# Residual and normalised activations on VectorE in 512-column pieces, with half units, ordered splits and paced scatters

## The chip, the cores and the metric

The kernel runs on one core of a Trainium2 chip. The metric is the device time of one execution in microseconds (us), the median of several runs; less is better. The engines are TensorE (PE; its weight loads are shown as PEld), VectorE (DVE), ScalarE (ACT), GpSimd (POOL) and SyncE (SP, which here only issues loads and stores). GpSimd issues DMAs too, among them all gathers and scatters by index.

## The reference

One decoder layer for 256 tokens of width 2048, with 16 learned meta tokens ahead of them (272 positions), all in float32:

```python
h = layer_norm(concat(meta, x))
proj = h @ w_in                      # 9264 columns: pool, z, x, B, C, dt
mix = concat(pool_mix(...), ssd_mix(...)) @ w_out
h = layer_norm(ALPHA * h + mix)
h = layer_norm(ALPHA * h + peer_ffn(h))

def peer_ffn(xb):                    # 16384 experts of one neuron
    q = (xb @ wq)                    # 8 heads, two halves of 128
    # top 16 of 128 keys per half, top 16 of the 256 pairs, softmax -> gate
    act = gelu(xb . u_tab[expert])
    return (gate * act) @ v_tab[expert]
```

The meta tokens are dropped from the output.

## The kernel before

Every large matrix product is done in three passes over pairs of fp32r numbers: each weight and each activation is split into a high part (a rounded copy) and a low part (the rest), and high x high, high x low and low x high are added up in PSUM. A weight unit is 128 x 1024 numbers. `next_unit` (L114) keeps three units ahead of the one in use: SP loads the raw unit (L124), ScalarE casts it to `wh` (L127), VectorE subtracts to get `wl` (L128). `raw`, `wh` and `wl` have three buffers each. W_ORDER (L79 to L109) is the list in which units come, and it must match the order of use. So each unit costs ScalarE and VectorE one instruction each, and TensorE waits if one of these is late.

The stages, with their places in the trace:

1. *Start (to about 25 us).* x is loaded and normalised without gain and bias (L198 to L231). For each of 16 chunks of 128 columns, TensorE transposes it and `normed_T` (L178) applies gain and bias and splits it into `hTH` and `hTL`: one or two instructions on ScalarE and one or two on VectorE per chunk.
2. *Input projection and mixers (to 506 us).* `mm_unit` (L251) multiplies half of the contraction (8 chunks, 24 matmuls) by one unit; `proj` (L259) calls it for both halves and after each half calls `tick`, which runs one step of the list `side`. All smaller work is written as generators on that list.
3. *Output projection (506 to 701 us).* `wide_pass` (L475) goes twice (dh) over 32 units, with 12 matmuls of 512 columns per unit. In the first pass, at unit 20, `w_out_body` (L506) loads the two norm vectors, broadcast to all partitions (1 MB each), and x again (two tiles `h`, 1 MB each), and rebuilds the normalised input as the residual: VectorE subtracts the mean and scales, GpSimd multiplies by the gain and adds the bias, each on a whole 128 x 2048 tile. Then it loads the vectors of the next norm into the same buffers:

```python
dve.tensor_scalar(h, h, mv_in[:, tt, 0:1], rs_in[:, tt:tt + 1], ALU.subtract, ALU.mult)
pool.tensor_mul(h, h, gb[0])
pool.tensor_add(h, h, gb[1])
```

4. *First LayerNorm (701 to about 740 us).* Statistics, scaling, then transposes and `normed_T` for 16 chunks into `h1H` and `h1L` (L568 to L572).
5. *Query projection (to 825 us)* with 16 pairs of units (L848); routing steps run from `side`. The first entry on it, `nat_steps` (L577), multiplies and adds gain and bias to the normalised tiles on GpSimd, whole tiles again, and stores them to `h1d` in DRAM from GpSimd's queue, for the last residual.
6. *u blocks (825 to 1607 us).* 128 blocks of 128 experts, two units each, Gelu, gating. The gating multiplies on GpSimd (L734). Three steps of `side` run per block until the routing is done; from then on the gating of the first half is spread over the blocks left to 62. Then the active rows of the coefficients are scattered to DRAM (`acd`) so that rows in use come close together: `scatter` (L690) is an indirect DMA on GpSimd, one per 128 experts, behind the last pinned instruction on that queue. From the time when positions are known, three of the other half (`scatter_0`) go out after each u block, beside those of the first half.
7. *Expert stage (1607 to 2112 us).* 107 blocks: two dense ones, whose coefficients stay in SBUF, and 105 that are read back. For each, `rows` (L952) loads a coefficient tile `ac` on SP and gathers 128 rows of v (1 MB) by index into `rawv` on GpSimd; the gather is pinned to program order. `rawv` has three buffers, `ac` seven. The halves of a row go through the same casts and subtractions as weights. `a_split` (L966) splits the coefficients on ScalarE and VectorE when a block comes up. A block multiplies both token tiles (24 matmuls) or one (12). After each of the early blocks, two more `scatter_0` are issued (L1057). `vp`, the pool of these buffers, is opened in the space of `ap1`, the half buffer `a_half[1]`, which is closed just ahead of it (L935). The residual is reloaded from `h1d` on GpSimd's queue before the stage (L933).

The framework orders the instructions of each engine by priority (the order of the program) and by when their operands are ready by its own model; an instruction named in `keep_in_program_order` keeps its place. Each engine then runs its list strictly in order, so one that waits holds up all behind it.

```python
while next_got[0] < min(i + 1 + GA, near[0]):
    k = next_got[0]
    half, blk, _ = V_BLOCKS[k]
    got[k], acs[k] = rows(acd[half][blk * P:(blk + 1) * P, :], "rawv", "ac", GA, GA + 4)
    next_got[0] += 1
```

## Time and profile before

| | |
|---|---|
| time, median of 3 runs | 2144.62 us (2144.24 to 2146.91) |
| profiled execution, its own time | 2123.32 us |
| its span, first to last instruction | 2121.6 us |
| mean granted TensorE clock | 0.982 |
| TensorE busy (matmuls) | 2031.5 us, 96%, 14780 instructions |
| VectorE | 1592.9 us, 75% |
| ScalarE | 1114.5 us, 53% |
| GpSimd | 570.7 us, 27% |
| HBM read and written | 407.2 and 21.1 MB, 202 GB/s over the span |

All rows come from one profiled execution. Busy time is an average over stages with different limits; what a change is worth is read in its own stage. A window gives the busy time of each engine in a stretch, with the number of instructions. In the timeline, neighbouring instructions of one kind are merged ("x4"), and the bracket gives the idle time of the engine before them and what ended it. Matmuls overlap, so the time of a group of them is longer than the step to the next group.

### The profile page before, as it was taken

The numbers are of one execution on the slowest core, as the hardware profiler recorded it, in microseconds if no ns is written. First come the engines' busy times: TensorE is split into PE (matmuls) and PEld (weight loads), VectorE is DVE, ScalarE is ACT, GpSimd is POOL, SyncE is SP. The second block draws the span as 40 slices with busy tenths as digits, with TensorE's granted clock in tenths as the row PEclk, the third lists the DMA queues.
The fourth block names the chain that finished last, engine by engine and source line by source line (L and its number), as shares of the span: only waits on it lengthen the run. The fifth ranks groups of instructions, "written<-read, shape, count | busy, mean of one in ns | idle before, by whom it ended". The sixth has DMA issues, their size and how long they took to land. (4 is left out here: it accounts for less than half of the span.)

```text
span 2121.6 us, 37592 instructions
## 1 busy us (share of the span) xinstructions
PE 2031.5 (96%) x14780; PEld 1867.4 (88%) x14780; DVE 1592.9 (75%) x2500; ACT 1114.5 (53%) x1637; POOL 570.7 (27%) x433
## 2 busy tenths in 40 slices
PE   7999999999899699999999999999997999998997
PEld 6999999998688599999999999999996778776775
DVE  7767777777654868999899879999754556565667
ACT  6457777776243444445558663333443445454553
POOL 1000000000400400000555426566275733222330
PEclk9999999999999799999999999999999999999999
DMA  5555555555566355555455556656687987677774
GB/s 174 183 175 175 175 175 175 175 175 196 212 202 196 116 187 180 176 182 180 151 168 171 168 179 195 200 182 206 203 263 255 306 304 282 245 271 265 268 271 156
DMA packets 113972, 430.76 MB, mean 203 GB/s; under 512 B 14113, under 2 KB 27809, under 8 KB 98801
## 3 DMA queue, kind: packets, MB, share of 16 engines
q1 hardware_dynamic: 88880, 280.19, 42.8%
q0 software_dynamic: 24624, 147.62, 19.3%
q8 instruction: 116, 1.90, 0.3%
q14 instruction: 64, 0.52, 0.1%
q10 hardware_dynamic: 288, 0.52, 0.1%
HBM read 407.20 MB, written 21.09 MB: 202 GB/s over the span
## 5 line engine op out<-in xcount | busy, mean ns | idle before, releaser
L127 ACT CAST wh<-raw 128x1024 fp32r<-128x1024 f32 (+1 forms) x502 | 525.5, 1047 | 668.8 <-PE psu L256 334.6
L128 DVE TENSOR_TENSOR wl<-raw,wh 128x1024 fp32r<-128x1024 f32 (+1 forms) x502 | 638.3, 1274 | 280.0 <-ACT wh L127 276.6
L989 PE MATMUL psv<-wh,v_scr 128*128 128x512 f32 x1304 | 365.1, 401 | 31.4 <-ACT wh L127 28.4
L128 DVE TENSOR_TENSOR wl<-rawv,wh 128x1024 fp32r<-128x1024 f32 x210 | 252.8, 1223 | 140.4 <-ACT wh L127 138.1
L734 POOL TENSOR_TENSOR o<-oe,gT 128x512 f16<-128x512 f16 x128 | 204.4, 1608 | 481.5 <-DVE gT L845 273.2
L989 PEld LDWEIGHTS psv<-wh,v_scr 128*128 128x128 f32 x1304 | 247.8, 191 | 96.5 <-ACT wh L127 36.1
L127 ACT CAST wh<-rawv 128x1024 fp32r<-128x1024 f32 x210 | 215.9, 1047 | 149.2 <-PE psv L989 90.1
L256 PE MATMUL psu<-h1H,wh 128*128 128x256 f32 x2048 | 292.9, 286 | 0.0
L256 PE MATMUL psu<-h1L,wh 128*128 128x256 f32 x2048 | 286.1, 282 | 0.0
L256 PE MATMUL psu<-h1H,wl 128*128 128x256 f32 x2048 | 284.4, 282 | 0.0
L256 PEld LDWEIGHTS psu<-h1H,wh 128*128 128x128 f32 x2048 | 261.5, 189 | 0.0
L256 PEld LDWEIGHTS psu<-h1L,wh 128*128 128x128 f32 x2048 | 261.4, 189 | 0.0
L256 PEld LDWEIGHTS psu<-h1H,wl 128*128 128x128 f32 x2048 | 261.0, 188 | 0.0
L956 POOL DMA_INDIRECT rawv<-in_v,ac x105 | 135.2, 1288 | 299.1 <-DVE wl L128 234.4
L989 PE MATMUL psv<-wl,v_scr 128*128 128x512 f32 x652 | 209.9, 401 | 1.0
L256 PE MATMUL psj<-hTH,wh 128*128 128x272 f32 (+5 forms) x1168 | 174.3, 292 | 0.0
L692 POOL DMA_INDIRECT acd<-a,flags x126 | 149.2, 1184 | 74.8 <-DVE a L595 32.5
L256 PE MATMUL psj<-hTH,wl 128*128 128x272 f32 (+5 forms) x1168 | 166.0, 284 | 0.0
L256 PE MATMUL psj<-hTL,wh 128*128 128x272 f32 (+5 forms) x1168 | 165.9, 284 | 0.0
L989 PEld LDWEIGHTS psv<-wl,v_scr 128*128 128x128 f32 x652 | 123.1, 191 | 36.5 <-DVE wl L128 8.6
L256 PEld LDWEIGHTS psj<-hTH,wh 128*128 128x128 f32 (+1 forms) x1168 | 152.9, 188 | 2.2
L256 PEld LDWEIGHTS psj<-hTL,wh 128*128 128x128 f32 (+1 forms) x1168 | 151.7, 187 | 0.1
(252 smaller groups left out, 2310.5 us busy)
## 6 DMA issues: line engine op xcount, KB each, us to landing
raw<-in_u SPq DMA_DIRECT2D x256, 512.0 KB, 4.0
raw<-in_w_in SPq DMA_DIRECT2D x144, 512.0 KB, 3.6
raw<-in_w_out SPq DMA_DIRECT2D x64, 512.0 KB, 4.2
raw<-in_wq SPq DMA_DIRECT2D x32, 512.0 KB, 3.8
ac<-acd SPq DMA_DIRECT2D x105, 128.5 KB, 4.5
clb<-cd POOLq DMA_DIRECT2D x8, 816.0 KB, 4.5
x<-in_x SPq DMA_DIRECT2D x4, 512.0 KB, 6.2
gb<-in_ln_nat POOLq DMA_DIRECT2D x2, 1024.0 KB, 6.8
```

Source lines behind the costliest of these rows:

```text
L127: act.copy(wh[:, :n], raw[:, :n])
L128: dve.tensor_sub(wl[:, :n], raw[:, :n], wh[:, :n].bitcast(F32))
L256: pe.matmul(ps[:m, :n], w[:, k * m:(k + 1) * m], xx[:, kh * 8 + k, t0:], start=first and k == 0, stop=last and k == 7)
L692: i = pool.indirect_dma_start(out=acd[half][:, :], out_offset=bass.IndirectOffsetOnAxis(ap=pos[half][:, b:b + 1], axis=0), in_=a_half[half ...
L734: behind[0] = pool.tensor_mul(o1, oe.unsqueeze(2).to_broadcast([P, 4, 2, 64]), gT[:, t0:t0 + 4, :].unsqueeze(3).to_broadcast([P, 4, 2, 64]))
L956: i = pool.indirect_dma_start(out=raw, out_offset=None, in_=v[:, :], in_offset=bass.IndirectOffsetOnAxis(ap=ac.bitcast(U32)[:, T:T + 1], a ...
L989: pe.matmul(po[tt][n], mm[:, tt * P:(tt + 1) * P], w[:, c:c + 512], start=first, stop=end)
```

## The change

Seven edits in one kernel.

- `w_out_body`: the residual is rebuilt on VectorE alone, by `h_steps`: two scalar_tensor_tensors on each of four pieces of 512 columns, for two tiles, one piece per tick. The loads of the next norm's vectors move from unit 20 to unit 31, behind a drain.
- `nat_steps`: multiply and add on VectorE in pieces of 512 columns, eight steps instead of four, and the stores to `h1d` go to SP's queue.
- Start: after chunk 7, the first halves of the dt unit and of two projections run, before the transposes of chunks 8 to 15; `proj` takes up their PSUM tiles from `pre`. The same after chunk 7 of the first LayerNorm, with the first halves of three query units (NQ1). W_ORDER follows.
- Scatters: from u block 123 on, `scatter_0` isn't called; in the expert stage it is called from block 2 on.
- Reloads of `h1d`: behind block 8 of the expert stage.
- `ac` loads: in a loop of their own, two blocks ahead of the gathers.
- `a_split`: for block i + 1 in block i, with both instructions pinned to program order.

```diff
-    W_ORDER = [w_dt[kh] for kh in range(2)]
-    W_ORDER += [w_in[j, kh] for j in range(72) for kh in range(2)]
+    W_ORDER = [w_dt[0], w_in[0, 0], w_in[1, 0], w_dt[1], w_in[0, 1], w_in[1, 1]]
+    W_ORDER += [w_in[j, kh] for j in range(2, 72) for kh in range(2)]
     W_ORDER += [w_out[k * P:(k + 1) * P, dh * 1024:(dh + 1) * 1024] for dh in range(2) for k in range(32)]
-    W_ORDER += [wq[j, kh] for j in range(16) for kh in range(2)]
+    W_ORDER += [wq[j, kh] for kh in range(2) for j in range(NQ1)]
+    W_ORDER += [wq[j, kh] for j in range(NQ1, 16) for kh in range(2)]
     W_ORDER += [u[b, kh] for b in range(P) for kh in range(2)]
...
+            if k == KC // 2 - 1:
+
+                for t0, m in ((0, NH), (14, P), (14, P)):
+                    ps = ps_tile("psj")
+                    mm_unit(ps, hTH, hTL, 0, m, L - t0, t0)
+                    pre.append((t0, ps))
...
-        ps = ps_tile("psj")
-        for kh in range(2):
-            mm_unit(ps, hTH, hTL, kh, m, L - t0, t0)
+        if pre:
+            was, ps = pre.pop(0)
+            assert was == t0
             tick()
+        else:
+            ps = ps_tile("psj")
+            mm_unit(ps, hTH, hTL, 0, m, L - t0, t0)
+            tick()
+        mm_unit(ps, hTH, hTL, 1, m, L - t0, t0)
+        tick()
         return ps
...
-    ps = ps_tile("psj")
-    for kh in range(2):
-        mm_unit(ps, hTH, hTL, kh, NH, L)
+    _, ps = pre.pop(0)
+    mm_unit(ps, hTH, hTL, 1, NH, L)
...
+    def h_steps(tt, h, gb):
+        for c in range(4):
+            cs = slice(c * 512, (c + 1) * 512)
+            dve.scalar_tensor_tensor(h[:, cs], h[:, cs], mv_in[:, tt, 0:1], gb[0][:, cs], ALU.subtract, ALU.mult)
+            dve.scalar_tensor_tensor(h[:, cs], h[:, cs], rs_in[:, tt:tt + 1], gb[1][:, cs], ALU.mult, ALU.add)
+            yield
...
-                dve.tensor_scalar(h, h, mv_in[:, tt, 0:1], rs_in[:, tt:tt + 1], ALU.subtract, ALU.mult)
-                pool.tensor_mul(h, h, gb[0])
-                pool.tensor_add(h, h, gb[1])
+                side.append(h_steps(tt, h, gb))
                 hs.append(h)
                 sts.append(lp.tile([P, 4, 6], F32, name=f"sts{tt}"))
+        if i == 31:
+            drain()
             for q in range(2):
-                gb1.append(lp.tile([P, D], F32, tag=f"gb{q}", name=f"g1b{q}"))
+                gb1.append(lnp[0].tile([P, D], F32, tag=f"gb{q}", name=f"g1b{q}"))
                 pool.dma_start(gb1[q], ln_nat[2 + q:3 + q, :].partition_broadcast(P))
...
+        if k == KC // 2 - 1:
+            for j in range(NQ1):
+                pre.append(ps_tile("psq1"))
+                mm_unit(pre[j], h1H, h1L, 0, P, T)
...
         for tt in range(2):
-            pool.tensor_mul(hs[tt], hs[tt], gb1[0])
-            yield
-            pool.tensor_add(hs[tt], hs[tt], gb1[1])
-            pool.dma_start(h1d[tt], hs[tt])
-            yield
+            for c in range(4):
+                cs = slice(c * 512, (c + 1) * 512)
+                dve.tensor_mul(hs[tt][:, cs], hs[tt][:, cs], gb1[0][:, cs])
+                dve.tensor_add(hs[tt][:, cs], hs[tt][:, cs], gb1[1][:, cs])
+                yield
+            nc.sync.dma_start(h1d[tt], hs[tt])
...
-        ps = ps_tile("psq1")
-        for kh in range(2):
-            mm_unit(ps, h1H, h1L, kh, P, T)
+        if j < NQ1:
+            ps = pre[j]
             tick()
+        else:
+            ps = ps_tile("psq1")
+            mm_unit(ps, h1H, h1L, 0, P, T)
+            tick()
+        mm_unit(ps, h1H, h1L, 1, P, T)
+        tick()
...
-            if pos[0] is not None:
+            if pos[0] is not None and b < 123:
                 for _ in range(3):
                     scatter_0()
...
-    for tt in range(2):
-        pool.dma_start(rr[tt], h1d[tt])
...
-        while next_got[0] < min(i + 1 + GA, near[0]):
-            k = next_got[0]
-            half, blk, _ = V_BLOCKS[k]
-            got[k], acs[k] = rows(acd[half][blk * P:(blk + 1) * P, :], "rawv", "ac", GA, GA + 4)
+
+        end = min(i + 1 + GA, near[0])
+        while next_ac[0] < min(end + 2, len(V_BLOCKS)):
+            half, blk, _ = V_BLOCKS[next_ac[0]]
+            assert half or n_sc[0] == HALF[0][1]
+            acs[next_ac[0]] = load_ac(acd[half][blk * P:(blk + 1) * P, :], "ac", GA + 4)
+            next_ac[0] += 1
+        while next_got[0] < end:
+            got[next_got[0]] = rows(acs[next_got[0]], "rawv", GA)
             next_got[0] += 1
         return got[i]
...
-    def rows(src, rtag, atag, rb, ab, pin=True):
-        ac = vp.tile([P, ROW], F32, tag=atag, name="ac", bufs=ab)
+    def load_ac(src, tag, bufs):
+        ac = vp.tile([P, ROW], F32, tag=tag, name="ac", bufs=bufs)
         nc.sync.dma_start(ac, src)
-        raw = vp.tile([P, D], F32, tag=rtag, name=rtag, bufs=rb)
+        return ac
+
+    def rows(ac, tag, bufs, pin=True):
+        raw = vp.tile([P, D], F32, tag=tag, name=tag, bufs=bufs)
         i = pool.indirect_dma_start(out=raw, out_offset=None, in_=v[:, :],
                                     in_offset=bass.IndirectOffsetOnAxis(ap=ac.bitcast(U32)[:, T:T + 1], axis=0))
         if pin:
             tc.keep_in_program_order(i)
             behind[0] = i
-        return raw, ac
+        return raw
...
-        split(ah[:, c], al[:, c], src[:, c])
-        return ah, al
+
+        tc.keep_in_program_order(act.copy(ah[:, c], src[:, c]))
+        tc.keep_in_program_order(dve.tensor_sub(al[:, c], src[:, c], ah[:, c].bitcast(F32)))
+        a_ops[i] = ah, al
...
-        ah, al = a_split(i) if what == "d" else (None, None)
+        if i == 0:
+            a_split(0)
+        if i + 1 < len(V_BLOCKS):
+            a_split(i + 1)
         for dh in range(2):
-            wh, wl = next_unit()
-            if ah is None:
-                ah, al = a_split(i)
-            ops = (ah, al, wh, wl)
+            ops = (*a_ops[i], *next_unit())
...
-        for _ in range(2):
+        for _ in range(2 if i > 1 else 0):
             scatter_0()
+        if i == 8:
+            for tt in range(2):
+                pool.dma_start(rr[tt], h1d[tt])
```

## Rows read from the trace of the kernel before

**Rows 1.** The page, parts 1 and 2: busy time of each engine; TensorE's clock by slice.

```profile
PE 2031.5 (96%) x14780; PEld 1867.4 (88%) x14780; DVE 1592.9 (75%) x2500; ACT 1114.5 (53%) x1637; POOL 570.7 (27%) x433
...
PEclk9999999999999799999999999999999999999999
```

**Rows 2.** Windows: stretch, length, busy us (instructions) by engine, clock, DMA share, GB/s.

```profile
520.00:549.00 29.00, 29.00 (x128) 23.98 (x129) 15.55 (x19) 12.56 (x15) 2.81 (x5) 1.00 0.83 312
738.00:760.00 22.00, 22.00 (x181) 22.00 (x180) 10.06 (x10) 9.96 (x13) 0.00 (x0) 0.96 0.62 196
1010.00:1210.00 200.00, 196.68 (x2005) 195.08 (x2004) 187.04 (x195) 130.50 (x254) 106.82 (x66) 0.99 0.54 164
```

**Rows 3.** Windows of the projection's matmuls alone (tile pso).

```profile
550.00:592.00 42.00, 31.02 (x110) 0.84 0.51 173
```

**Rows 4.** Timelines, output projection: start, us, engine, line, out<-in, count [idle before].

```profile
551.01 5.52 POOL L520 TENSOR_TENSOR h<-h,gb 128x2048 f32<-128x2048 f32 x1 [26.34 <-DVE h L519]
...
557.53 18.80 DVE L128 TENSOR_TENSOR wl<-raw,wh 128x1024 fp32r<-128x1024 f32 x5
584.26 3.73 DVE L128 TENSOR_TENSOR wl<-raw,wh 128x1024 fp32r<-128x1024 f32 x3 [7.92 <-ACT wh L127]
...
563.11 2.07 PE L482 MATMUL pso<-wl,mixH 128*128 128x512 f32 x4 [5.21 <-DVE wl L128]
```

**Rows 5.** Timeline of the first LayerNorm.

```profile
697.09 0.68 DVE L548 SCALAR_TENSOR_TENSOR h<-h,pso 128x512 f32<-128x512 f32 x1
...
713.52 9.18 POOL L579 TENSOR_TENSOR h<-h,g1b 128x2048 f32<-128x2048 f32 x2 [11.58 <-PE pst L571]
713.60 9.38 DVE L187 TENSOR_TENSOR h1L<-full,h1H 128x256 fp32r<-128x256 f32 x2
...
722.67 9.39 POOL L581 TENSOR_TENSOR h<-h,g1b 128x2048 f32<-128x2048 f32 x2
```

**Rows 6.** Windows of the query projection's matmuls alone (tile psq).

```profile
701.50:740.10 38.60, 12.07 (x64) 0.69 0.24 87
740.10:760.00 19.90, 19.70 (x166) 1.00 0.59 185
```

**Rows 7.** Window of TensorE at the start.

```profile
11.00:24.60 13.60, 13.23 (x48) 1.00 0.38 133
```

**Rows 8.** Windows of the expert stage's matmuls alone (tile psv).

```profile
1607.00:1640.00 33.00, 20.91 (x78) 0.84 0.74 262
1640.00:1840.00 200.00, 196.51 (x836) 1.00 0.83 289
...
1860.00:1950.00 90.00, 87.40 (x362) 1.00 0.75 265
1950.00:1970.00 20.00, 13.29 (x47) 0.74 0.61 208
1970.00:2090.00 120.00, 115.19 (x483) 0.99 0.80 284
```

**Rows 9.** Timeline, start of the expert stage.

```profile
1608.04 0.42 DVE L595 TENSOR_TENSOR a_dense<-a,psu 128x256 f32<-128x256 f32 x1
...
1614.45 80.72 SPq L954 DMA_DIRECT2D ac<-acd  x22
...
1618.04 0.64 PE L989 MATMUL psv<-wl,v_scr 128*128 128x512 f32 x2
...
1630.06 2.93 PE L989 MATMUL psv<-wh,v_scr 128*128 128x512 f32 x6 [11.38 <-ACT wh L127]
```

**Rows 10.** Waits of the expert stage: engine, line, waited for, us, times, longest.

```profile
ACT v_scr L175 <- DMA ac<-acd: 82.7, 28, 10.5
...
ACT wh L127 <- DMA rawv<-in_v,ac: 56.3, 33, 4.4
...
PE psv L989 <- ACT wh L127: 28.4, 15, 11.4
```

**Rows 11.** DMA issues, 1500 to 1700 us: the gathers, median us to landing.

```profile
rawv<-in_v,ac POOLq DMA_INDIRECT x18, 8.4
```

More of the change, by code (lines that the diff above doesn't have):

```diff
@@ L24 @@
 NL1 = 3
+NQ1 = 3
 NLB = 4
@@ L195, in tile_layer, with mm_unit @@
     hTL = hTp.tile([P, KC, L], F32R, name="hTL")
+    def mm_unit(ps, xh, xl, kh, m, n, t0=0):
+        wh, wl = next_unit()
+        for w, xx, first, last in ((wh, xh, kh == 0, False), (wh, xl, False, False), (wl, xh, False, kh == 1)):
+            for k in range(8):
+                pe.matmul(ps[:m, :n], w[:, k * m:(k + 1) * m], xx[:, kh * 8 + k, t0:],
+                          start=first and k == 0, stop=last and k == 7)
+    pre = []
     with tc.tile_pool(name="ln0", bufs=1) as lp:
@@ L249, in tile_layer @@
     pool.memset(ones, 1.0)
-    def mm_unit(ps, xh, xl, kh, m, n, t0=0):
-        wh, wl = next_unit()
-        for w, xx, first, last in ((wh, xh, kh == 0, False), (wh, xl, False, False), (wl, xh, False, kh == 1)):
-            for k in range(8):
-                pe.matmul(ps[:m, :n], w[:, k * m:(k + 1) * m], xx[:, kh * 8 + k, t0:],
-                          start=first and k == 0, stop=last and k == 7)
     def proj(t0, m=P):
-        ps = ps_tile("psj")
-        for kh in range(2):
-            mm_unit(ps, hTH, hTL, kh, m, L - t0, t0)
+        if pre:
+            was, ps = pre.pop(0)
+            assert was == t0
             tick()
+        else:
[4 more added lines that the diff above has]
+        tick()
         return ps
@@ L941, in tile_layer @@
     next_got = [NDB]
+    next_ac = [NDB]
     def gathered(i):
-        while next_got[0] < min(i + 1 + GA, near[0]):
-            k = next_got[0]
-            half, blk, _ = V_BLOCKS[k]
-            got[k], acs[k] = rows(acd[half][blk * P:(blk + 1) * P, :], "rawv", "ac", GA, GA + 4)
+        end = min(i + 1 + GA, near[0])
[6 more added lines that the diff above has]
+            got[next_got[0]] = rows(acs[next_got[0]], "rawv", GA)
             next_got[0] += 1
         return got[i]
-    def rows(src, rtag, atag, rb, ab, pin=True):
-        ac = vp.tile([P, ROW], F32, tag=atag, name="ac", bufs=ab)
+    def load_ac(src, tag, bufs):
+        ac = vp.tile([P, ROW], F32, tag=tag, name="ac", bufs=bufs)
         nc.sync.dma_start(ac, src)
-        raw = vp.tile([P, D], F32, tag=rtag, name=rtag, bufs=rb)
+        return ac
+    def rows(ac, tag, bufs, pin=True):
+        raw = vp.tile([P, D], F32, tag=tag, name=tag, bufs=bufs)
         i = pool.indirect_dma_start(out=raw, out_offset=None, in_=v[:, :],
@@ L960, in rows @@
             behind[0] = i
-        return raw, ac
+        return raw
     near = [len(V_BLOCKS)]
     a_n = [0]
+    a_ops = {}
     def a_split(i):
@@ L999, in v_rest @@
                 for tt, first in ((0, e - s), (1, nblk - s)):
-                    raw, ac = rows(acd[half][bass.ds(i * P + first * P, P), :], "rawl", "acl", 1, 1, False)
+                    ac = load_ac(acd[half][bass.ds(i * P + first * P, P), :], "acl", 1)
+                    raw = rows(ac, "rawl", 1, False)
                     ah, al = (v_scr[:, 2 * tt + q, tt * P:(tt + 1) * P] for q in range(2))
@@ L1045, in tile_layer @@
                 gb2.append(g2)
-        ah, al = a_split(i) if what == "d" else (None, None)
+        if i == 0:
+            a_split(0)
+        if i + 1 < len(V_BLOCKS):
+            a_split(i + 1)
         for dh in range(2):
-            wh, wl = next_unit()
-            if ah is None:
-                ah, al = a_split(i)
-            ops = (ah, al, wh, wl)
+            ops = (*a_ops[i], *next_unit())
             if i not in LATE:
```

## The prediction

> **What bounds the kernel now.** I read the busy shares of the engines and the granted clock first [rows 1]. TensorE is busy for 96% of the span, and its granted clock is below nine tenths in one of 40 slices only. [...] Next I counted matmuls in stretches: a stretch in which TensorE never waits gives the dense rate, and the count missing elsewhere gives the loss with the slow clock included.
>
> The output projection runs 128 matmuls in 29 undisturbed us, 4.4 per us [rows 2]. From 550 to 592 us it holds 110 [rows 3] where 42 us would take 185: 75/4.4 = **17.0 us lost**. The timeline shows why [rows 4]: while GpSimd runs 128x2048 multiplies and adds of some 5.5 us each, five weight splits on VectorE take 18.80 us together, where three take 3.73 a little later. TensorE waits 5.21 us for one of them and restarts at half speed (2.07 us for four matmuls, where four dense ones need 0.9).
>
> At the first LayerNorm the pattern is plainer [rows 5]. GpSimd's two multiplies and two adds (9.18 and 9.39 us) each hold up a pair of VectorE subtractions (9.38 us for two). The window from 701.5 to 740.1 us holds 64 matmuls; at the 166 per 19.9 us behind it, 64 take 7.7 us [rows 6]. **30.9 us are lost**, of which 2 x 9.3 = 18.6 lie under GpSimd's four instructions; the rest is the chain through statistics, transposes and evictions, and a cold restart.
>
> At the start TensorE is busy 13.23 of the 13.6 us before its first projection [rows 7]: little to win.
>
> In the expert stage 836 matmuls fill 196.5 busy us, 4.25 per us [rows 8]. Each row less its count/4.25 gives the loss: 33 - 78/4.25 = 14.6 us at its start (1607 to 1640), 3.3 us to 1840, 4.8 us (1860 to 1950), 8.9 us (1950 to 1970), 6.4 us (1970 to 2090). At its start [rows 9] the first coefficient load (ac) is issued at 1614.45 us and the first gathered matmul comes at 1630.06, after 11.38 us of waiting. Later ScalarE waits for ac loads with its splits, 82.7 us in 28 waits, and the weight casts queue behind it; TensorE's own waits for casts sum to 28.4 us [rows 10].
>
> **The change part by part.**
>
> *Residual preparation (w_out_body, h_steps).* Two VectorE tensor_scalars and four GpSimd instructions go; 16 scalar_tensor_tensors on 128x512 come, at 0.68 us as that form took [rows 5]: 10.9 us on VectorE. One tick per weight unit brings two, 1.36 us, beside a split of about 1.2 in the 2.7 us of a unit (12 matmuls at 4.4 per us). That is 95% if the pieces stay where they are emitted; hoisted earlier they meet a VectorE busy 15.55 of 29 us [rows 2]. The two norm-vector loads (1 MB each) move eleven units later on GpSimd's queue and meet the weight loads there; 520 to 549 us bore 4 MB of such loads beside dense matmuls [rows 2], so I cost them at nothing, and at 3 us if the weight prefetch runs dry. Of 17.0 us I expect **16** back (13 to 17).
>
> *First LayerNorm.* nat_steps on VectorE, 16 pieces at 0.68 = 10.9 us over the first eight query units, where VectorE idles 12 of 22 us [rows 2]. The 18.6 us of blocking go, less the 1 us or so that the subtractions need themselves. Three half units (72 matmuls, 72 x 0.12 = 8.6 us) can run while chunks 8 to 15 are evicted, which fills 1 to 3 us more. **19** (15 to 22). The two stores of h1d move to SP's queue, two issues there; the weight loads behind them may start late, by nothing up to 3 us, inside the lower end.
>
> Cutting is itself charged. The row gives 0.68 us for 512 columns. [...] The idle VectorE time in [rows 2] covers the 22 us of pieces in my sum; without the cover 22 us return.
>
> *Ticks.* nat_steps takes eight ticks where it took four, so at three per block the gating starts 4/3 blocks later, and the same steps fall on fewer blocks, with VectorE already busy 187 of 200 us [rows 2]. Cost 0 to 3; I take **-1**.
>
> *Start.* Dense TensorE leaves nothing: **0**. Bounds +2, and -4 if casts for the next units, waiting for a weight buffer, stand before evictions of chunks 8 to 15 on ScalarE.
>
> *Expert stage, start.* With b < 123, 15 scatters (five blocks, three each) leave the end of the u blocks, and the two reloads (rr, 2 MB) wait until block 8, so the first half's last scatter follows its own block and no longer a queue. But the gather buffers lie in the space of the half buffer that the last u block still reads, at 1608.04 us [rows 9]. From the first ac issue to the first gathered matmul it takes 15.6 us now, with rr beside; from 1608.5 that is 1624, or 1622 without rr, against dense matmuls that end at 1618.7. The wait shrinks from 11.4 to some 4 us: with the slow restart after it **8** of 14.6 (5 to 14).
>
> *Expert stage, rest.* The ac loads go out two blocks earlier on SP and the splits stay in program order on ScalarE and VectorE, a block ahead: no cast stands behind a split whose load is late. Of 4.8 + 8.9 + 6.4 = 20.1 us I take **14** (8 to 19); the rest stays because a gather lands in 8.4 us [rows 11] and ScalarE waits 56.3 us for gathers too [rows 10]. Fifteen more scatters and the rr reload, 4 MB, now pass at 0.83 DMA share: at the row's 289 GB/s 14 us of transfer, against a headroom of 0.17 x 90 us = 15 over the 21 blocks in which they pass (18 matmuls on average, 4.3 us) [rows 8]. Cost 0 to 6, **-3**; nothing below zero is excluded, since the same scatters leave before block 49 in both kernels.
>
> **Sum**: 16 + 19 - 1 + 0 + 8 + 14 - 3 = 53 us. The profiled execution took 2123.3 us, 21.3 us (1.0%) less than the median of the runs, 2144.6; nothing in its trace says where the runs lose that. Profiled: 2070; against the median: 2144.6 - 53 = **2091.6**, say 2091.
>
> **Rivals.**
>
> *Gathers set the pace.* The waits for ac go, but TensorE meets waits for gathers instead: for it, the 8.4 us landing beside 2.8 us for a one-sided block (12 matmuls), and the 56.3 us; against it, those waits seldom reach TensorE now. The stage then yields 5 at its start and loses the 3: 16 + 19 - 1 + 5 - 3 = 36, 2109 us. Chance 0.2.
>
> *VectorE fills up.* The pieces become ready together when their loads land and run as blocks in front of splits (8 x 0.68 = 5.4 us, twice a stage). For it: 95% occupancy by emission; against: the gaps in [rows 2]. Half of 35 is lost: 53 - 17 = 36, 2109 us. Chance 0.1.
>
> *Slower.* Pinned splits turn into the wait themselves: each split must follow program order on two engines, so ScalarE stops at it in every block. Price: the mean wait, 82.7/28 = 2.95 us, in 105 blocks, of which 28.4/82.7 reaches TensorE, is 106 us, in place of the 28.4 us that stand there now. The other parts give 34, so the net is 106 - 28 - 34 = 44 us slower, 2189. It decides from (34 + 28)/105 = 0.6 us of TensorE waiting per block. Against it: with the split a block ahead and ac two blocks earlier its operand has landed before the cast's own gather. Chance 0.05.
>
> *It does not do what it says.* The framework orders instructions by readiness; the half units may change nothing. That costs 0 to 3 us of the 19, inside the forecast. That nothing at all changes has 0.02: GpSimd's long instructions are gone whatever the order.
>
> **How the numbers follow.** The forecast's own case has 0.63. All lower bounds: 13 + 15 - 3 - 4 + 5 + 8 - 6 = 28, 2117 us. All upper: 17 + 22 + 2 + 14 + 19 = 74, 2071. Both extremes at once are unlikely, but the runs' 21 us above the profile is unexplained and may not return in full, so I put the low end at 2064 and the high end at 2115, which takes in the first two rivals. A measurement of this kernel tells about 0.2% (4.3 us) from no change. Faster 0.93, within it 0.02, slower 0.05.
>
> **What would show it.** Right: no GpSimd instruction of 4 us or more in the output projection and LayerNorm, subtractions at 0.4 us, 550 to 592 us at 4.4 matmuls per us; query matmuls dense by about 722; a first gathered matmul within 6 us of the dense blocks' last one; ScalarE's waits for ac near zero. Wrong: TensorE waits for casts behind gathers as large as now, splits delayed in rows of pieces, or a gap between chunks 7 and 8 at the start.

## The result and the profile after

The changed kernel takes 2090.36 us (median, 2082.15 to 2096.47), before 2145.76 in the same comparison: a ratio of 0.9739, interval 0.9704 to 0.9774. The forecast was 2091. The sum came out, but its terms did not all: two were too small in opposite directions. So the hit to within 1 us is in part luck. The 21 us that the profiled execution of before lacked most likely have a cause of their own, which the profile after shows. One execution in the record that is set apart as slow, one of e7's four below, is left out of its median.

The page of the changed kernel, parts 1 and 2, to be set beside [rows 1]:

```profile
PE 2025.3 (97%) x14780; PEld 1868.7 (90%) x14780; DVE 1571.0 (75%) x2530; ACT 1116.7 (53%) x1637; POOL 525.2 (25%) x423
...
PEclk9999999999999999999999999999989999999999
```

Shares hardly move: 97% for 96%. The answers are in the stages.

**Output projection**, its matmuls alone, the stretch that answers to [rows 3] (the stage begins 3.3 us later):

```profile
553.00:595.00 42.00, 40.87 (x181) 1.00 0.70 237
```

181 matmuls where 110 were, at a clock of 1.00: 181/42 = 4.3 per us, nearly the dense 4.4. GpSimd runs nothing here but its DMA issues.

**First LayerNorm.** VectorE's timeline, then the query projection's windows, for [rows 5] and [rows 6]:

```profile
691.75 0.68 DVE L607 TENSOR_TENSOR h<-h,g1b 128x512 f32<-128x512 f32 x1
...
698.38 1.09 DVE L189 TENSOR_TENSOR h1L<-full,h1H 128x256 fp32r<-128x256 f32 x3
...
704.50 0.68 DVE L607 TENSOR_TENSOR h<-h,g1b 128x512 f32<-128x512 f32 x1
```

```profile
688.60:712.90 24.30, 13.30 (x83) 0.79 0.21 65
712.90:732.00 19.10, 19.10 (x163) 1.00 0.86 291
```

Three subtractions take 1.09 us where two took 9.38. The loss between the stages is 24.3 - 83/8.34 = 14.3 us, where it was 30.9. The first row of the timeline shows something that stands in the way of more: eight pieces of the residual run between 691.75 and 706.1 us, inside the chain of statistics, transposes and evictions, 8 x 0.68 = 5.4 us of VectorE. How much of it TensorE pays for is open; its waits for the scaled tiles there sum to 5.3 us, where before has 4.1.

**Start.** TensorE's timeline:

```profile
19.48 2.38 PE L204 MATMUL psj<-hTH,wh 128*48 128x272 f32 x8 [0.20 <-ACT hTH L185]
...
22.15 2.77 PE L204 MATMUL psj<-hTH,wh 128*128 128x258 f32 x11 [0.29 <-ACT wh L129]
...
37.14 1.93 PE L204 MATMUL psj<-hTH,wh 128*48 128x272 f32 x13 [0.65 <-ACT hTH L185]
```

The dense stretch of [rows 7] now has waits, two for evictions and one for a cast of weights for the half units. The output projection begins at 509.8 us, 3.3 later than the 506.5 of before.

**u blocks**, the 130 us in which the gating begins. The window of TensorE's u matmuls in the changed kernel, then the same stretch of before, counted from the first u matmul (150 to 280 us behind it):

```profile
945.80:1075.80 130.00, 113.56 (x915) 0.99 0.52 156
```

```profile
975.50:1105.50 130.00, 121.02 (x974) 0.99 0.54 165
```

59 matmuls fewer. At the 8.2 per us of the 150 us ahead of it (1222 matmuls in both kernels) that is 7.2 us lost. TensorE's waits over the u blocks name the place:

```profile
PE pg L772 <- DVE o L757: 10.3, 8, 2.4
```

```profile
PE pg L745 <- DVE o L730: 4.2, 5, 2.4
```

The gating's matmuls wait for VectorE eight times, 10.3 us in all; before (second row) they wait five times, 4.2 us.

**Expert stage**, the stage's matmuls in five windows from their first one (after, then before; [rows 8] had other cuts):

```profile
1603.40:1643.40 40.00, 35.25 (x145) 0.96 0.87 293
1643.40:1723.40 80.00, 78.69 (x335) 1.00 0.97 322
1723.40:1843.40 120.00, 117.84 (x499) 0.99 0.79 284
1843.40:1963.40 120.00, 119.28 (x511) 1.00 0.83 289
1963.40:2076.20 112.80, 110.61 (x472) 1.00 0.71 253
```

```profile
1607.20:1647.20 40.00, 28.11 (x109) 0.87 0.71 250
1647.20:1727.20 80.00, 76.57 (x322) 1.00 0.93 314
1727.20:1847.20 120.00, 118.35 (x508) 1.00 0.75 266
1847.20:1967.20 120.00, 109.86 (x442) 0.95 0.73 258
1967.20:2110.50 143.30, 138.49 (x580) 0.98 0.70 249
```

With each row's length less count/4.25 as its loss, before loses 14.4, 4.2, 0.5, 16.0 and 6.8 us, after 5.9, 1.2, 2.6, -0.2 and 1.7: 41.9 against 11.2. The start of the stage on the timeline, for [rows 9], and its waits, for [rows 10]:

```profile
1603.16 1.15 POOL L1105 DMA_DIRECT2D rr<-h1d  x2 [8.72 <-PE psu L204]
...
1604.66 32.91 SPq L990 DMA_DIRECT2D ac<-acd  x12
...
1612.49 1.00 POOL L995 DMA_INDIRECT rawv<-in_v,ac  x1 [8.19 <-DMA ac<-acd]
...
1619.51 3.41 PE L1032 MATMUL psv<-wh,v_scr 128*128 128x512 f32 x8 [4.75 <-ACT v_scr L1019]
```

```profile
ACT wh L129 <- DMA rawv<-in_v,ac: 74.6, 38, 10.1
...
PE psv L1032 <- ACT v_scr L1019: 6.6, 5, 4.8
```

The first ac load goes out at 1604.66 us, right behind the last u block, 1.3 us behind the stage's first matmul (1603.4) where before has 7.2 (1614.45 and 1607.2); from there to the first gathered matmul it takes 14.9 us (15.6 before), and the wait is 4.75 us where it was 11.38. The first row is a surprise: the residual's reload (rr) still goes out at the head of the stage. The program calls it behind block 8, but its tile is free and the framework lists it early, so this edit moved nothing. ScalarE's waits for ac, 82.7 us before, have no row any more. It still waits 74.6 us for gathers, but TensorE has no row of waiting for casts any more. Its longest row for the stage, for splits, sums to 6.6 us, and 4.75 of that is the wait at the start.

**A stretch of gaps.** At 1531 to 1561 us, in the last u blocks, the changed kernel shows something that no row of before has. Windows of all engines (columns as in [rows 2]), then TensorE's and GpSimd's timelines:

```profile
1521.00:1531.00 10.00, 10.00 (x86) 10.00 (x86) 4.44 (x6) 3.10 (x5) 7.50 (x8) 1.00 0.89 249
1531.00:1561.00 30.00, 23.34 (x109) 19.99 (x108) 5.57 (x6) 5.85 (x7) 23.31 (x21) 0.71 0.54 176
```

```profile
1532.78 0.63 PE L204 MATMUL psu<-h1H,wh 128*128 128x256 f32 x4 [0.17 <-issue]
1534.21 0.63 PE L204 MATMUL psu<-h1H,wh 128*128 128x256 f32 x4 [0.80 <-issue]
1535.64 0.52 PE L204 MATMUL psu<-h1L,wh 128*128 128x256 f32 x3 [0.80 <-issue]
```

```profile
1533.32 0.96 POOL L719 DMA_INDIRECT acd<-a,flags  x1 [0.30 <-issue]
1534.59 1.79 POOL L719 DMA_INDIRECT acd<-a,flags  x1 [0.30 <-issue]
```

109 matmuls run in 30 us where 8.6 per us would make 258: 17 us lost. TensorE stops after four matmuls for 0.8 us, for nothing that the profile shows, and its granted clock falls to 0.71. GpSimd issues scatters back to back all the while. The stretch ends when their run ends. TensorE is not the only engine that is late. ScalarE's cast and VectorE's subtraction of one unit in this stretch, then in the second execution of the same kernel, e2 below, which has no gaps:

```profile
1531.40 1.05 ACT L129 CAST wh<-raw 128x1024 fp32r<-128x1024 f32 x1 [3.96 <-remote]
...
1534.32 1.23 DVE L130 TENSOR_TENSOR wl<-raw,wh 128x1024 fp32r<-128x1024 f32 x1 [5.63 <-issue]
```

```profile
1530.35 1.05 ACT L129 CAST wh<-raw 128x1024 fp32r<-128x1024 f32 x1 [1.53 <-PE psu L204]
...
1531.43 1.23 DVE L130 TENSOR_TENSOR wl<-raw,wh 128x1024 fp32r<-128x1024 f32 x1 [1.29 <-ACT wh L129]
```

VectorE starts 1.87 us behind the end of the cast, and again the profile shows nothing that it waits for; in e2 it starts 0.03 us behind.

### The profile page after: what moved, and what is told of

The parts are those of the page before. It is cut to its first block, busy times and chain, and to the rows that moved or that the text cites. A ratio compares the mean times of both kernels' runs of the same rounds, so it can differ in the third digit from the quotient of the medians.

```text
span 2087.7 us, 37525 instructions
## 1 busy us (share of the span) xinstructions
PE 2025.3 (97%) x14780; PEld 1868.7 (90%) x14780; DVE 1571.0 (75%) x2530; ACT 1116.7 (53%) x1637; POOL 525.2 (25%) x423
## 5 line engine op out<-in xcount | busy, mean ns | idle before, releaser
L130 DVE TENSOR_TENSOR wl<-raw,wh 128x1024 fp32r<-128x1024 f32 (+1 forms) x502 | 624.4, 1245 | 298.6 <-ACT wh L129 268.1
L129 ACT CAST wh<-rawv 128x1024 fp32r<-128x1024 f32 x210 | 220.3, 1049 | 205.0 <-PE psv L1032 126.9
L204 PE MATMUL psu<-h1L,wh 128*128 128x256 f32 x2048 | 290.5, 284 | 3.8 <-issue 3.7
L204 PE MATMUL psu<-h1H,wl 128*128 128x256 f32 x2048 | 288.6, 284 | 0.0
L995 POOL DMA_INDIRECT rawv<-in_v,ac x105 | 127.3, 1212 | 256.1 <-DVE wl L130 200.0
L719 POOL DMA_INDIRECT acd<-a,flags x126 | 154.5, 1226 | 99.4 <-DVE a L622 58.7
L204 PEld LDWEIGHTS psj<-hTH,wl 128*128 128x128 f32 (+1 forms) x1168 | 151.6, 187 | 0.0
```

Source lines behind the costliest of these rows:

```text
L129: act.copy(wh[:, :n], raw[:, :n])
L130: dve.tensor_sub(wl[:, :n], raw[:, :n], wh[:, :n].bitcast(F32))
L204: pe.matmul(ps[:m, :n], w[:, k * m:(k + 1) * m], xx[:, kh * 8 + k, t0:], start=first and k == 0, stop=last and k == 7)
L719: i = pool.indirect_dma_start(out=acd[half][:, :], out_offset=bass.IndirectOffsetOnAxis(ap=pos[half][:, b:b + 1], axis=0), in_=a_half[half ...
L995: i = pool.indirect_dma_start(out=raw, out_offset=None, in_=v[:, :], in_offset=bass.IndirectOffsetOnAxis(ap=ac.bitcast(U32)[:, T:T + 1], a ...
```

## The experiments

They ran in three groups of four; each group shares its runs of the kernel before (2122.4, 2150.6 and 2147.7 us) and its chip: e1 to e4 ran on chip 11 by the record, e5 to e8 on 13, e9 to e12 on 7. For the first pair no chip is on record. Every stage length below is that of one execution. Stage lengths come from the profile of each run: from the start of the first matmul of a tile to that of its last one; "in" is the time from the span's start to the first matmul of the output projection, "LN+q" from that projection's last to the query projection's last. us less than before compares medians in the same group.

| run | in | output proj. | LN+q | u | expert | gaps | less than before | ratio (interval) |
|---|---|---|---|---|---|---|---|---|
| before | 506.5 | 194.7 | 124.1 | 780.9 | 503.3 | no | | |
| after | 509.8 | 178.8 | 107.0 | 806.8 | 472.8 | yes | 55.4 | 0.9739 (0.9704 to 0.9774) |
| e1 before again | 507.5 | 192.5 | 122.1 | 779.4 | 503.8 | no | 5.3 | 0.9978 (0.9952 to 1.0003) |
| e2 after again | 510.3 | 179.2 | 107.1 | 788.4 | 477.3 | no | 49.7 | 0.9761 (0.9734 to 0.9788) |
| e3 no start units | 507.8 | 179.3 | 106.3 | 785.7 | 472.7 | no | 51.0 | 0.9771 (0.9751 to 0.9792) |
| e4 one scatter | 510.2 | 178.2 | 105.6 | 788.6 | 489.7 | no | 35.7 | 0.9838 (0.9820 to 0.9857) |
| e5 four ticks | 510.1 | 178.6 | 106.3 | 798.7 | 477.7 | yes | 66.0 | 0.9695 (0.9645 to 0.9745) |
| e6 scatters back | 510.6 | 178.7 | 107.0 | 819.7 | 472.5 | yes | 45.2 | 0.9787 (0.9746 to 0.9828) |
| e7 not pinned | 509.5 | 181.2 | 105.8 | 815.6 | 503.7 | yes | 27.0 | 0.9818 (0.9743 to 0.9892) |
| e8 old splits | 509.8 | 178.9 | 106.7 | 811.7 | 507.7 | yes | 29.5 | 0.9840 (0.9794 to 0.9886) |
| e9 GpSimd back | 509.8 | 191.5 | 115.9 | 801.0 | 475.7 | yes | 40.6 | 0.9817 (0.9781 to 0.9854) |
| e10 no half units | 504.0 | 178.1 | 107.9 | 810.8 | 471.5 | yes | 54.7 | 0.9758 (0.9728 to 0.9789) |
| e11 own block | 511.4 | 178.9 | 106.1 | 806.2 | 611.0 | yes | -84.2 | 1.0402 (1.0369 to 1.0434) |
| e12 combined | 507.8 | 178.1 | 107.2 | 799.1 | 477.4 | yes | 64.8 | 0.9705 (0.9679 to 0.9731) |

**e1, e2: both kernels again, unaltered.**

> The kernel before, unaltered, with a new profile. Theory A: the u blocks hold a stall of about 17 us while GpSimd issues scatters back to back; it is there in most executions of either kernel and was missing in the one execution of before that was profiled (2123 us against 2144 timed). Then this profile comes near 2144, and its u blocks (first to last matmul) take 795 to 800 us instead of 779.0. Theory B: the stall belongs to the changed kernel; then the u blocks take 779 again, and where this profile is longer the time lies elsewhere.

> The changed kernel, unaltered, with a new profile. Theory A (a stall that comes and goes between executions): the u blocks take either about 788 or about 805 us, and the total moves with them. Theory B (the change causes it): 805 us again, with TensorE's gaps beginning near the same block. Both: about 2090 timed.

In this group the kernel before takes 2122.4 us where it took 2145.8, the changed one 2072.7 where it took 2090.4, and no profile of the group has the gaps. The changed kernel in e2, all engines, in the run of scatters:

```profile
1520.00:1560.00 40.00, 40.00 (x339) 40.00 (x339) 20.80 (x30) 16.61 (x22) 29.21 (x27) 1.00 0.90 268
```

27 GpSimd instructions at the same cadence, and 339 matmuls in 40 us. So the same program has the gaps in one execution and not in another: theory B falls as it stood. Theory A holds in its core (788.4 us without, 806.8 with), but not as it was put: e1's profile is 2119, not 2144, since its group had none. In the other two groups, where before takes 2148 to 2151 us, all eight profiles have the gaps. Chip and occasion change together here, so the record can't tell which of them brings the gaps. The u blocks of e2 are still 9 us longer than those of e1: that part is the change's.

**e3: no early half units at the start.**

```diff
-            if k == KC // 2 - 1:
-                for t0, m in ((0, NH), (14, P), (14, P)):
-                    ps = ps_tile("psj")
-                    mm_unit(ps, hTH, hTL, 0, m, L - t0, t0)
-                    pre.append((t0, ps))
```

> The changed kernel without the three early half units at the start (input order of weights as before). My reading of the two traces: the early units cost 3.3 us, since TensorE was dense there and now waits twice more; then the input projection ends near 503.3 us instead of 506.7 and the time is 2087. Rival: they gain what the forecast's bound of +2 allowed; then 2092.

The output projection begins at 507.8 us, 2.5 earlier than in e2. The total is 1.2 us less than e2's, below what this measurement tells; the stage shows that the units at the start cost some 2.5 us.

**e4: one scatter per u block.**

```diff
-            if pos[0] is not None and b < 123:
-                for _ in range(3):
+            if pos[0] is not None:
+                for _ in range(1):
...
-        for _ in range(2 if i > 1 else 0):
+        for _ in range(3 if i > 1 else 0):
```

> The changed kernel with one scatter of the first half per u block instead of three, up to the last u block, and three per block in the expert stage instead of two, from block 2 on. If the run of scatters back to back is what holds TensorE up near 1531 to 1562 us, that stall goes: 17 us, less 0 to 6 for some twenty scatters more in the expert stage, 2073 to 2079. If the stall has nothing to do with the scatters, it stays and the time is 2090 to 2096.

It says nothing about the gaps, as its group had none. It prices scatters in the expert stage: 51 there instead of 40, and 489.7 us against 477.3 in e2. The loss lies at 40 to 120 us into the stage (16.7 us, 4.9 in e2). The windows of all engines there, e4, then e2:

```profile
1623.50:1703.50 80.00, 68.62 (x269) 52.81 (x268) 37.29 (x42) 31.75 (x42) 62.63 (x58) 0.94 0.86 274
```

```profile
1625.90:1705.90 80.00, 76.75 (x319) 60.72 (x318) 45.33 (x51) 39.29 (x51) 59.56 (x52) 0.98 0.95 312
```

GpSimd is busy 62.63 us with 58 instructions, and 58 gaps of 0.30 between them make 17.4 more: it is full. The DMA share falls from 0.95 to 0.86 at the same time. With three scatters per block GpSimd's issuing sets the pace of the gathers, not the transfers. With two (52 x 0.30 + 59.56 = 75 of 80 us) it just fits.

**e5: four ticks for the residual, not eight.**

```diff
                 dve.tensor_add(hs[tt][:, cs], hs[tt][:, cs], gb1[1][:, cs])
-                yield
+                if c % 2:
+                    yield
```

> The changed kernel with the normalised residual's multiplies and adds handed out two pieces of 512 columns at a time, in four steps of the side list as before, not eight. Theory: the u blocks grew from 780 us in both profiles of before to 788 because routing ends later and the gating falls on fewer blocks; four steps bring the u blocks back to about 780 and the time to 8 us less than the changed kernel, 58 below before. Rival: the growth has another cause (the order of VectorE's list); the u blocks stay at 788 and the time at 50 below before.

The stretch 150 to 280 us behind the first u matmul, again TensorE's u matmuls:

```profile
945.10:1075.10 130.00, 121.19 (x986) 1.00 0.54 167
```

And TensorE's waits for the gating over the u blocks:

```profile
PE pg L773 <- DVE o L758: 3.7, 4, 2.4
```

986 matmuls, as many as e1's 987 and against 915 in the changed kernel, and four waits where the changed kernel has eight. That window shows the ticks' 7 to 8 us. The u blocks take 798.7 us with the gaps, where five executions with the changed kernel's u blocks and gaps (the first, e7, e8, e10, e11) take 806.2 to 815.6. The whole is 66.0 us under before in its group, where theory gave 58 and the changed kernel had 55.4 in another; the stage length is the better measure.

**e6: scatters back where they were.**

```diff
-            if pos[0] is not None and b < 123:
+            if pos[0] is not None:
...
-        for _ in range(2 if i > 1 else 0):
+        for _ in range(2):
```

> The changed kernel with the pacing of scatters undone (three per u block up to the last, two per block of the expert stage from the first); the reload of the residual stays behind block 8. By the forecast: fifteen scatters back in the u blocks return 3 us of the later stage, but the first gathers queue behind them and lose about 5 of the 8 us won at the start; 2 us slower, 48 below before. Rival, from the run with one scatter per block, where 15 us went on the expert stage: a scatter there costs 0.5 to 0.7 us wherever it stands, fifteen fewer give 8 to 10 us back, and the kernel is faster, 53 to 56 below before.

The u blocks take 819.7 us. Their last stretch, all engines:

```profile
1531.00:1600.00 69.00, 56.86 (x314) 50.11 (x315) 19.05 (x22) 16.88 (x21) 45.32 (x40) 0.78 0.57 178
```

The gaps go on with the longer run of scatters. Against e2's 788.4 us they cost 31.3 us here and, in the five executions with the changed kernel's u blocks, 18 to 27. The expert stage is as short as with pacing (472.5 us, 25 scatters in it; 472.8 with 40), and its first 40 us lose 5.9 us in both. But that is no test of the pacing at the stage's start, as the gaps gave GpSimd time to finish. GpSimd and SP in e6, then in e1, which has before's scatters and no gaps:

```profile
1606.82 0.97 POOL L719 DMA_INDIRECT acd<-a,flags  x1 [4.79 <-DVE a L622]
...
1618.12 19.71 SPq L990 DMA_DIRECT2D ac<-acd  x9
```

```profile
1606.99 0.97 POOL L692 DMA_INDIRECT acd<-a,flags  x1 [0.30 <-DMA acd<-a,flags]
...
1609.75 14.55 SPq L954 DMA_DIRECT2D ac<-acd  x8
```

In e6 the last scatter goes out 10 us ahead of the expert stage's first matmul (1616.8 us) and the first ac load follows the last u block. In e1 the last one goes out at 1606.99 us, 4.6 us behind the stage's first matmul (1602.4), and the ac load goes out behind it, 7.4 us into the stage. In e2, paced and without gaps either, it goes out 1.3 us into the stage (1585.9):

```profile
1587.17 20.63 SPq L990 DMA_DIRECT2D ac<-acd  x9
```

**e7, e8: splits not pinned; splits and loads as they were.** e7 keeps the split a block ahead:

```diff
-        tc.keep_in_program_order(act.copy(ah[:, c], src[:, c]))
-        tc.keep_in_program_order(dve.tensor_sub(al[:, c], src[:, c], ah[:, c].bitcast(F32)))
+        split(ah[:, c], al[:, c], src[:, c])
```

e8 also takes the split back into its own block and drops the lead of the loads:

```diff
-        while next_ac[0] < min(end + 2, len(V_BLOCKS)):
+        while next_ac[0] < min(end, len(V_BLOCKS)):
...
-        if i + 1 < len(V_BLOCKS):
-            a_split(i + 1)
+        ah, al = a_split(i) if what == "d" else (None, None)
         for dh in range(2):
-            ops = (*a_ops[i], *next_unit())
+            wh, wl = next_unit()
+            if ah is None:
+                ah, al = a_split(i)
+            ops = (ah, al, wh, wl)
```

> The changed kernel with the coefficients' splits a block ahead, but left to the framework's order (not pinned). If being a block ahead is what counts, the expert stage stays at 473 to 477 us. If the pinning is, the framework puts splits in front of casts again, ScalarE waits for coefficient loads as before, and the stage grows by 5 to 15 us.

> The changed kernel with each block's split where it was (in its own block, not pinned) and the coefficient loads no longer two blocks ahead; scatters paced as changed. The forecast gave 14 us for these two edits together: the expert stage goes from about 475 to 489, 36 below before. Rival: the stage's gain of 28 us comes from the pacing and the later reload alone; then it stays near 475.

Without the pin the expert stage takes 503.7 us, as much as before, and e8 adds only 4 to that. Each is the figure of one execution; the timed ones of e7 that count run from 2103 to 2130 us, and the profile is of the longest, as it is in e8. The waits of e7's expert stage:

```profile
ACT v_scr L177 <- DMA ac<-acd: 68.8, 23, 7.3
...
PE psv L1031 <- ACT wh L129: 26.3, 17, 4.2
```

These are [rows 10] again: 68.8 us of ScalarE's waits for ac (82.7 before) and 26.3 of TensorE's for casts (28.4). Being a block ahead in the program does nothing while the framework may order the splits anew.

**e9: the multiplies and adds on GpSimd again.**

```diff
-                side.append(h_steps(tt, h, gb))
+                dve.tensor_scalar(h, h, mv_in[:, tt, 0:1], rs_in[:, tt:tt + 1], ALU.subtract, ALU.mult)
+                pool.tensor_mul(h, h, gb[0])
+                pool.tensor_add(h, h, gb[1])
...
-                dve.tensor_mul(hs[tt][:, cs], hs[tt][:, cs], gb1[0][:, cs])
-                dve.tensor_add(hs[tt][:, cs], hs[tt][:, cs], gb1[1][:, cs])
+            pool.tensor_mul(hs[tt], hs[tt], gb1[0])
+            pool.tensor_add(hs[tt], hs[tt], gb1[1])
```

> The changed kernel with the residual's multiplies and adds on whole tiles again (one VectorE and two GpSimd instructions per tile in the output projection, two GpSimd per tile behind the first LayerNorm, stores from GpSimd's queue); half units kept. Theory: GpSimd's long instructions hold up VectorE, so the output projection goes from 179 back to 193 to 195 us, and the step from its end to the query projection's end from 107 to 120 to 124 us. Rival for the second: the half units cover it, then 110. The u blocks lose their eight ticks and with them 8 us, as in the run with four ticks.

191.5 us for the output projection, 12.7 more than with the change, and 115.9 for LN+q, 8.9 more. VectorE's timeline:

```profile
560.62 17.68 DVE L130 TENSOR_TENSOR wl<-raw,wh 128x1024 fp32r<-128x1024 f32 x4
...
723.97 8.84 DVE L189 TENSOR_TENSOR h1L<-full,h1H 128x256 fp32r<-128x256 f32 x2
```

The blocked subtractions are back as in [rows 4] and [rows 5], and beside the two VectorE instructions ahead of them and the stores' queue nothing else was put back in these stages. They are the cause: the subtractions take 4.42 us each, where 1.23 and 0.42 are usual in this trace. By what route GpSimd's instructions hold them up was not shown. LN+q stays under the 122 to 124 us of before; the half units, the main part of the change that is left in this stage, then fill some 6 to 8 us, by this difference and not by a run of their own.

**e10: no half units, loads not ahead.** As e3, and

```diff
-        if k == KC // 2 - 1:
-            for j in range(NQ1):
-                pre.append(ps_tile("psq1"))
-                mm_unit(pre[j], h1H, h1L, 0, P, T)
...
-        while next_ac[0] < min(end + 2, len(V_BLOCKS)):
+        while next_ac[0] < min(end, len(V_BLOCKS)):
```

> The changed kernel without half units, at the start and behind the first LayerNorm, and with coefficient loads no longer two blocks ahead of the gathers; splits stay pinned a block ahead. The three places lie in stages of their own. Start: input projection ends 2.5 to 3.5 us earlier, as without the early units before. LayerNorm: 1 to 3 us longer than 107 by the forecast. Expert stage: if the early loads count, it grows from 475 by 3 to 10; if pinning alone does, it stays within 2 us.

The output projection begins at 504.0 us, 5.8 before the changed kernel's 509.8 (e3 had 2.5; the start varies by some us between executions). LN+q is 107.9, 0.9 more than the changed kernel's, and 0.7 to 2.3 more than in all runs that keep the half units and VectorE's pieces (105.6 to 107.2 there): without GpSimd's blocking the half units have little to fill. The expert stage takes 471.5: the early loads bring nothing that shows.

**e11: pinned, but in its own block.**

```diff
-        if i + 1 < len(V_BLOCKS):
-            a_split(i + 1)
+        ah, al = a_split(i)
         for dh in range(2):
-            ops = (*a_ops[i], *next_unit())
+            ops = (ah, al, *next_unit())
```

> The changed kernel with pinned splits, but each at the start of its own block and not a block ahead. Rival of the forecast (pinned splits become the wait themselves): ScalarE stops at each split, TensorE waits 0.6 us or more in each of 105 blocks, and the expert stage grows from 475 to 535 us or more. If the pinning alone brings the gain, the stage stays at 473 to 478.

611.0 us, 138 more than the changed kernel, and the whole is slower than before by 84.2. One row of the stage's waits:

```profile
PE psv L1032 <- ACT v_scr L1019: 106.1, 100, 10.2
```

TensorE waits for the split 100 times, 1.06 us on average. The slower rival's mechanism is real; the lead of one block is what keeps it away.

**e12: the parts that paid, together.** As e3 and e5, and

```diff
-            if pos[0] is not None and b < 123:
-                for _ in range(3):
+            if pos[0] is not None and b < 127:
+                for _ in range(2):
```

> The changed kernel without half units at the start, with four steps instead of eight for the normalised residual, and with two scatters per u block to the 127th block instead of three to the 123rd (about as many in all). Theory: 3 us from the start, 8 from the ticks, and, where executions have TensorE's gaps while scatters go back to back, up to 17 more since GpSimd now idles between them; where they have none, nothing more. 61 to 78 us below before. Rival: the gaps come whatever the distance of the scatters; 61 below before at most.

64.8 us under before, 10 better than e10 in the same group (2082.9 against 2093.0), with u blocks of 799.1 us, gaps included. The scatters were not spread, GpSimd's timeline shows:

```profile
1520.49 1.48 POOL L715 DMA_INDIRECT acd<-a,flags  x1 [0.30 <-issue]
1522.27 0.97 POOL L715 DMA_INDIRECT acd<-a,flags  x1 [0.30 <-issue]
```

The framework lists those of later blocks early, since their data are ready, and GpSimd runs them back to back whatever the block in which the program calls them. So whether a slower cadence avoids the gaps wasn't tried, and the rival's 61 us was passed by 4 only.

## Why the prediction came out

Both reruns without gaps (e1 to e2) give each term cleanly; the pair of first profiles stands behind it.

| term | forecast | e1 to e2 | before to after |
|---|---|---|---|
| start | 0 (-4 to +2) | -2.8 | -3.3 |
| output projection | 16 (13 to 17) | 13.3 | 15.9 |
| first LayerNorm | 19 (15 to 22) | 15.0 | 17.1 |
| ticks | -1 (-3 to 0) | -9.0 | -25.9, of it gaps 17 to 18 |
| expert stage, start | 8 (5 to 14) | 7.3 | 8.5 |
| expert stage, rest, less scatters | 14 - 3 = 11 | 19.2 | 22.0 |

The expert stage's start is the gain in matmuls over its first 40 us by 4.25 (112 to 143, 109 to 145), the rest the gain in length less that. The e1 to e2 column sums to 43.0, and the spans differ by 2117.3 - 2074.7 = 42.6; the medians of that group by 49.7, or by 44.5 if e1's own ten executions stand for before. The forecast's 53 less its errors is thus 43 to 50 without gaps. That the timed gain of the first comparison was 55.4, and 2091 met to within 1 us, needs the gaps, which cost the kernel before more (below) and for which the forecast had no term: this part is luck, and so is that ticks and expert stage missed in opposite directions.

- **Residual preparation** was right in cause (e9) and size. The pieces took 0.67 to 0.75 us each, and no wait of VectorE's reached TensorE. Cutting is charged, as the forecast says: in before's trace VectorE's subtraction takes 0.287 us for 128 columns, 0.421 for 256 and 1.223 for 1024 (v_scr and wl from rawv), by which a cut costs some 0.15 us (2 x 0.287 - 0.421), an estimate.
- **First LayerNorm**: the blocking went as forecast. The 1 to 3 us for the half units were about 1 (e10), and 5.4 us of pieces that the forecast laid over the first eight query units stood inside the LayerNorm's own chain. That may be where the lower end comes from, but no run moved them: VectorE idle time behind the stage doesn't help if the framework puts the pieces ahead of it. The forecast's sign "dense by about 722" takes only the 18.6 us of blocking off the 740.1 of before; its own sum, with the 16 us of the output projection, gives 705, and it was 712.9.
- **Ticks**: the mechanism was right and the size wrong by a factor of seven (the window) to nine (the stage). The forecast let the same steps fall on fewer blocks, "with VectorE already busy 187 of 200 us", and took 1 us. In the blocks where the gating begins, its matmuls wait for VectorE up to 2.4 us each time; fewer blocks made eight such waits of five and 7.2 us in one window, and four ticks gave them back (e5).
- **Start**: the forecast said that a dense TensorE leaves nothing and gave a bound of -4 for casts ahead of evictions. The loss came, -2.5 to -3.3 (e3), inside that bound, but its mechanism is only partly seen: TensorE's rows there show 0.8 us of waits for evictions and 0.3 for a cast.
- **Expert stage, start**: 8 forecast, 7.3 to 8.5 measured, and the wait of 4.75 us (4.11 in e2) against "some 4". The step went as put, the first ac load right behind the last u block because no scatter stands ahead of it (1.3 us into the stage in e2, 7.4 in e1, behind a scatter), with two limits. The reload that the forecast also took from there never moved, and the pacing alone was not shown by a run, since e6 ran with gaps and e1 and e2 differ in every edit.
- **Expert stage, rest**: ScalarE's waits for ac were the cause, and the price of 14 was too low, because it kept 6 us for gathers. These waits grew (56.3 to 74.6 us), and TensorE's waits for casts, 28.4 us before, went all the same. Pinning and the block's lead are needed together (e7, e11); the loads' lead is not (e10).
- **Scatters**: the forecast priced them by DMA headroom, fifteen more. It was eleven more (40 against 29), and the resource is GpSimd's issue time (e4), which two per block still leave free.
- **The 21 us between profile and median**: left unexplained in the forecast. The gaps fit: before takes 2122 us in the group without them and 2148 to 2151 in those with them, and e6 with before's run of scatters loses 31 us to them. The mean granted clock that is on record for every timed execution of before points the same way: 0.980 to 0.985 in the first group, 0.972 to 0.982 in the other two. No execution of before with the gaps was profiled, so for before this is argued. Where there are gaps the pacing gives 4 to 14 us by moving scatters out of the u blocks: 819.7 in e6 against 806.2 to 815.6, or 4 to 8 against e7 and e8 of its own group. By the medians the gaps cost before 23 to 28 us and the changed kernel 18, so some 6 us of the first comparison's 55 come from them.

The rivals: gathers did not set the pace; VectorE filled up only inside the LayerNorm and where the gating begins (5.4 us of its time and 7.2 us lost, where its rival had 17 lost); part of the change did not do what it says (the reload, the lead of the loads), at no cost; and the slower case lies one edit away (e11).

## What to carry to other kernels

Where an instruction that waits for a load holds up others behind it (in before's expert stage ScalarE idles 9.26 us for the ac of a split, and three casts follow right behind it from 1962.10 us), issue it a block ahead and hold it there: here the lead without the pin was worth next to nothing (4 us), the pin without the lead cost 138 us, both together gave 26 to 31. Elementwise work taken from one engine has to be looked for in the chain of the other: ask not only whether VectorE has idle time but where the framework's order will put the pieces, and count the steps that a shared work list takes. Where a profiled execution is 1% faster than the timed ones, profile again before working with its sum.

## What was not expected of the hardware

While GpSimd issues scatters back to back (most of them 0.97 us, 0.30 apart), TensorE in some executions stops for 0.8 us after every few matmuls without a visible cause, at a granted clock of 0.71 over 30 us, and loses 18 to 27 us, or 31 where the run is longer. VectorE is held up with it: in the changed kernel's first profile its four splits in that stretch start 1.84 to 1.87 us behind their casts, in before and e2 splits start 0.03 behind. The same program in another execution went through the same scatters with 339 matmuls in 40 us. The changed kernel's first profile and all of e5 to e12 have it; before's profile and all of e1 to e4 have not, so it goes with the occasion of the run or with the chip (none of the four profiles on chip 11, all four on 13 and all four on 7) rather than with the kernel. That the scatters cause it is not shown, since runs of them as long or longer (49 in before's profile) pass without gaps. What TensorE waits for there is open.
